# Half of a 31-tap depthwise convolution moved from TensorE to VectorE in a two-layer hybrid block

## The chip, the core and the metric

The kernel runs on one core of a Trainium2 chip. The metric is the time of one execution on the device, in microseconds. A core has five instruction queues that run side by side, each strictly in the order in which its instructions stand: TensorE (PE, matrix products into PSUM; PEld is its weight load), VectorE (DVE), ScalarE (ACT), GpSimd (POOL) and SyncE (SP, which here only issues DMAs). An instruction waits at the head of its queue until what it needs is there, and everything behind it in that queue waits too.

## The reference, cut to what matters

Two layers over 256 tokens of width 1024. Each layer projects the normed input once, runs three branches (differential attention, a convolution branch, a gated delta rule in chunks), gates and adds them, and projects back to the width. The branch that the change touches is

```
u = a * sigmoid(g)                                # a, g: (256, 1024) each, from the input projection
u = causal_depthwise_conv(u, dw_w) + dw_b         # 31 taps, one filter per channel
u = layer_norm(u, ln_w, ln_b)
u = silu(u) * silu(z)
return u @ w_o
```

The convolution of one channel is `out[t] = b + sum over s of w[30-s] * u[t-s]`, for shifts s from 0 to 30. With channels on the 128 partitions and the 256 tokens along the free dimension, a shift is a slice.

## The kernel before, in words

Every projection is a "group" of 512 output columns. A group's weights come as four chunks of 512 KB (`load_chunk`, line 292): one DMA into `w_raw`, then ACT rounds it to `w_hi` (line 303) and DVE forms the remainder `w_lo` (line 304), since a product is made of three passes, hi·hi, hi·lo and lo·hi. Three buffers each of `w_raw`, `w_hi` and `w_lo` rotate. A group has eight k-steps, two per chunk. In `group_a` (channels on the partitions, line 355) a k-step is twelve matmuls of 256 columns, in `group_b` (line 318) six of 512. PSUM accumulators named `acc` rotate through four buffers, two for a group, so that a group can start only when the last but one has been read out.

The order on PE is the order in which the code is written: after each k-step, `pump` (line 270) lets the next due piece of a side stream run (the delta rule's small matmuls, transposes, attention scores). When a piece is due is reckoned by `clk`, a sum of assumed PE times. The other engines' order is made by a scheduler from priorities: `load_chunk` and side streams are raised (`high_priority`), other work stands in program order.

`SEQ` (line 59) lists the groups at the start of a layer: `v` values, `k` delta keys, `c` the convolution's two input groups, `q` and `w` delta queries and values, `d` a convolution group, `x` the start of the delta rule's last stream, `a` attention queries and keys, `z` a gate. The delta rule of one half of the heads (`hs` 0 or 1) has these pieces that appear below: `vp` (three DVE results that PE multiplies with `sel`, lines 667 to 688), the recurrence `dn_z`, `dn_t` (lines 690 to 697), `gf` (line 714), and in `dn_queries` the squares `gx` of the queries, summed by PE against `ones` (line 749), which need both halves of the query group's read-out (`evac_dn`, lines 598 to 608; `big` at line 608 is its end).

The convolution before is done on PE alone. `c_groups(s)` makes `u` for 512 channels in `c_u` and stores it to DRAM (`u_keep`); `conv_load(n)` brings diagonal tap matrices `wd` and four shifted copies `u4` for 256 channels; `conv_group(n)` (line 890) runs 64 small matmuls for each of two blocks of 128 channels into one `acc` tile, and ACT adds the bias on the way to `c_acc` (line 898). There are four such groups in a layer: `d0` and `d1` between the delta groups, `d2` before the last attention groups, and the fourth after the delta rule's output.

Of the kernel before, what the change touches and what calls it, by code (L numbers as in the profile page):

```python
# [10 lines left out]
F32 = mybir.dt.float32  # L11
# [3 lines left out]
AF = mybir.ActivationFunctionType  # L15
ALU = mybir.AluOpType
# [3 lines left out]
P = 128  # L20
T = 256
D = 1024
KT = D // P
GW = 512
DEPTH = 2
# [30 lines left out]
FINE = False  # L56
AHEAD = 600
W_AHEAD = 340
SEQ = "v0 k0 t0 v1 k1 c0 q0 w0 d0 x0 q1 w1 d1 x1 a0 c1 z0 z1 d2 a1".split()
TAPQ = 8  # L60


PC_DB, PC_LW, PC_LB, PC_SC, PC_SUB, PC_DNW = 0, 8, 16, 24, 120, 121
PC_N = 122
PR_AL, PR_DT, PR_LAM = 0, 8, 16
PR_N = 272
CO_ID, CO_NW, CO_TRI, CO_BDU, CO_OFF, CO_BD, CO_E16, CO_IF = 0, 128, 144, 272, 400, 528, 536, 552
# [21 lines left out]
def kernel(  # L89
# [13 lines left out]
    nc = tc.nc  # L103
    V, S, G, TE = nc.vector, nc.scalar, nc.gpsimd, nc.tensor
# [41 lines left out]
        return ap.unsqueeze(1).to_broadcast([ap.shape[0], n, ap.shape[1]])  # L146

    x_keep = dram.tile([T, D], F32, name="x_keep")
    u_keep = dram.tile([D, T], F32, name="u_keep")

    def big():
        return act.tile([P, 2, D], F32, name="big", bufs=3)
# [136 lines left out]
            yield 1.9  # L289

    counter = [0]
    def load_chunk(l, g, c):
        with tc.high_priority(offset=AHEAD + 400 if counter[0] == 0 else W_AHEAD):
            raw = wpool.tile([P, KC, GW], F32, name="w_raw", bufs=3)
            with tc.issue_after(x_dma[1].ins) if counter[0] < NCH else ExitStack():
                nc.sync.dma_start(out=raw, in_=wts[l, g, c])
            hi = wpool.tile([P, KC, GW], F32R, name="w_hi")
            lo = wpool.tile([P, KC, GW], F32R, name="w_lo")
            eng = G if POOL[counter[0] % (NG * NCH)] == "1" else V
            cuts = [slice(k, k + 1) for k in range(KC)] if counter[0] == 0 else [slice(0, KC)]  # L300
            counter[0] += 1
            for kk in cuts:
                S.copy(out=hi[:, kk], in_=raw[:, kk])  # L303
                eng.tensor_sub(out=lo[:, kk], in0=raw[:, kk], in1=hi[:, kk].bitcast(F32))  # L304
        return hi, lo
# [12 lines left out]
    def group_b(l, key, xs, evac, need=()):  # L318
        parts = load_group(l, ORDER.index(key))
        ps = [acc_tile() for _ in range(2)]  # L320
        for k in range(KT):
            for s in need:
                if k == 4 * s[0]:
                    finish(s[1])
            for t in range(2):
                step_b(xs, parts[k // KC], ps, k, t)
            if k == KT - 1:
                evac(ps)
            pump()

    def group_out(l, xs, evacs, need, split):
        parts = {}
# [22 lines left out]
    def group_a(l, key, xs, evac, need=()):  # L355
        xh, xl = xs
        parts = load_group(l, ORDER.index(key))
        ps = [acc_tile().rearrange("p (f t) -> p f t", f=2) for _ in range(2)]
        for c, (hi, lo) in enumerate(parts):
            for kk in range(KC):  # L360
                k = c * KC + kk
                for s in need:
                    if k == 4 * s[0]:
                        finish(s[1])
                for f in range(4):
                    o = ps[f // 2][:, f % 2, :]
                    fs = slice(f * P, (f + 1) * P)
                    last = k == KT - 1 and f % 2 == 1
                    mm(0.108, out=o, lhsT=hi[:, kk, fs], rhs=xh[:, k, :],
                       start=(k == 0 and f % 2 == 0), stop=False)  # L370
                    mm(0.108, out=o, lhsT=hi[:, kk, fs], rhs=xl[:, k, :],
                       start=False, stop=False)
                    mm(0.108, out=o, lhsT=lo[:, kk, fs], rhs=xh[:, k, :],
                       start=False, stop=last)
                    if FINE and f == 1:
                        pump()
                if k == KT - 1:
                    evac(ps)
                pump()

    def transpose4(src, tile_):
        tp = h4(tile_)
# [58 lines left out]
    for l in range(DEPTH):  # L441
# [10 lines left out]

        wbs = lay.tile([P, KT, 32], F32R, name="wbs")
        scw = pc[:, PC_SC:PC_SC + 96]
        ln2 = lay.tile([P, 16], F32, name="ln2")
        ln4 = lay.tile([P, 16], F32, name="ln4")
        nwc = lay.tile([P, 2], F32, name="nwc")
# [15 lines left out]
        def params():  # L473
            V.tensor_scalar(out=scw, in0=scw, scalar1=0.5, scalar2=None, op0=ALU.mult)
            S.copy(out=wbs[:, :, 0:16], in_=wb)
            V.tensor_sub(out=wbs[:, :, 16:32], in0=wb, in1=wbs[:, :, 0:16].bitcast(F32))
            if l == 0:
                masks()
            V.tensor_scalar(out=ln2, in0=pc[:, PC_LW:PC_LW + 16], scalar1=0.5, scalar2=None, op0=ALU.mult)
            V.tensor_scalar(out=ln4, in0=pc[:, PC_LW:PC_LW + 16], scalar1=0.25, scalar2=None, op0=ALU.mult)  # L480
            V.tensor_scalar(out=nwc[:, 0:1], in0=pc[:, PC_SUB:PC_SUB + 1], scalar1=1.0 - lambda_init,
                            scalar2=0.5, op0=ALU.mult, op1=ALU.mult)
            V.tensor_scalar(out=nwc[:, 1:2], in0=pc[:, PC_DNW:PC_DNW + 1], scalar1=0.5, scalar2=None,
                            op0=ALU.mult)
            lamp = sm.tile([P, 2, 64], F32, name="dn_t1", bufs=1)
            lamv = lamr.rearrange("p (a b d) -> p a b d", a=2, b=2)
            V.tensor_tensor(out=lamp, in0=lamv[:, :, 0, :], in1=lamv[:, :, 1, :], op=ALU.mult)
            lams = sm.tile([P, 2], F32, name="lams", bufs=1)
            V.tensor_reduce(out=lams, in_=lamp, axis=AX.X, op=ALU.add)
            lame = sm.tile([P, 2], F32, name="lame", bufs=1)  # L490
            S.activation(out=lame, in_=lams, func=AF.Exp)
            V.tensor_sub(out=nlam, in0=lame[:, 1:2], in1=lame[:, 0:1])
            V.tensor_scalar(out=nlam, in0=nlam, scalar1=-lambda_init, scalar2=None, op0=ALU.add)
# [359 lines left out]
        us = []  # L853

        def c_groups(s):
            tgs = []

            def evac_g(ps):
                for f in range(2):
                    tg = wc()  # L860
                    V.tensor_tensor(out=tg, in0=ps[f], in1=bc_mid(rnb, 2), op=ALU.mult)
                    S.activation(out=tg, in_=tg, func=AF.Tanh, scale=0.5)
                    V.scalar_tensor_tensor(out=tg, in0=tg, scalar=1.0, in1=bc_mid(rnb, 2),
                                           op0=ALU.add, op1=ALU.mult)
                    tgs.append(tg)

            def evac_u(ps):
                u = wk.tile([P, 4, T], F32, name="c_u", bufs=2)
                for f in range(2):
                    ins = V.tensor_tensor(out=u[:, 2 * f:2 * f + 2, :], in0=tgs[f], in1=ps[f],  # L870
                                          op=ALU.mult)
                us.append(u)
                return ins

            group_a(l, ("in", CG + s * GW), H, evac_g)
            group_a(l, ("in", CA + s * GW), H, evac_u)
            nc.sync.dma_start(out=u_keep[s * GW:(s + 1) * GW].rearrange("(a p) t -> p a t", p=P), in_=us[s])
            conv_load(2 * s)

        ac = act.tile([P, 8, T], F32, name="c_acc")  # L880

        def conv_load(n):
            with tc.high_priority(offset=W_AHEAD):
                nc.sync.dma_start(out=wd.rearrange("p f q j c -> p (f q j c)"), in_=cwd[l, n])
                for i in range(4):
                    nc.sync.dma_start(
                        out=u4[32 * i:32 * i + 32, :, i:T],
                        in_=u_keep[n * 2 * P:(n + 1) * 2 * P, 0:T - i].rearrange("(g c) t -> c g t", c=32))

        def conv_group(n):  # L890
            ps = acc_tile().rearrange("p (f t) -> p f t", f=2)
            for f in range(2):
                ct = 2 * n + f
                for q in range(TAPQ):
                    for j in range(4):
                        mm((T - 4 * q) / 2400.0, out=ps[32 * j:32 * j + 32, f, 4 * q:T], lhsT=wd[:, f, q, j, :],
                           rhs=u4[:, 4 * f + j, 0:T - 4 * q], start=(q == 0), stop=(q == TAPQ - 1))
                S.activation(out=ac[:, ct, :], in_=ps[:, f, :], func=AF.Identity, scale=0.5,  # L898
                             bias=pc[:, PC_DB + ct:PC_DB + ct + 1])
                pump()  # L900
            if n in (0, 2):
                conv_load(n + 1)

        def q_group(hs):
            group_a(l, ("in", DQ + hs * GW), H, evac_dn(hs, 1, sts[hs]["kq"][:, :, 1, :]))
# [247 lines left out]
        yc = []  # L1153

        def ln_stream():
            yield 18.6
            pmu = side_tile()
            rsum = gx().rearrange("p (a b) d -> p a (b d)", a=2)
# [184 lines left out]
```

## Time and profile before

| | us |
|---|---|
| median of 3 runs (lowest to highest) | 1106.14 (1105.72 to 1110.63) |
| the profiled execution, its own time | 1110.02 |
| its span | 1108.2 |
| PE busy in the span | 1061.9 |
| DVE busy | 805.4 |
| ACT busy | 550.3 |

The span is the stretch from the first to the last recorded instruction; the 1.8 us beside it lie around it. A row of a timeline gives start, length, engine, line, operation, output and inputs, shapes and count, and in brackets how long the engine had been idle before it and what ended the wait. A row with a count covers several instructions that follow each other closely; its length is from the first start to the last end.

### The profile page before, as it was taken

How to read it: one execution, taken by the hardware profiler on the slowest of the kernel's cores; microseconds unless marked ns; L12 is line 12 of the kernel's file. 1: busy time of each engine (PE TensorE's matmuls, PEld its weight loads, DVE VectorE, ACT ScalarE, POOL GpSimd, SP SyncE). 2: the span in 40 equal slices, each digit the busy share in tenths (PEclk: the TensorE clock that was granted, in tenths of full speed). 3: DMA queues.
4: the chain of work that ended last, by engine and by line, in shares of the span. 5: the costliest groups of instructions: out<-in, count | busy, mean ns of one | idle time of the engine just before them, and what ended most of it. 6: DMA issues, size and time to landing. Idle time of an engine off the chain costs nothing.

```text
span 1108.2 us, 18945 instructions
## 1 busy us (share of the span) xinstructions
PE 1061.9 (96%) x7396; PEld 920.1 (83%) x7396; DVE 805.4 (73%) x1610; ACT 550.3 (50%) x995; POOL 108.0 (10%) x74
## 2 busy tenths in 40 slices
PE   5998899999999999999999989999999999999996
PEld 4998898899687778897889988988987877889785
DVE  4889977586767656687677988767766775757965
ACT  4754544343656544545466534443346564544643
POOL 1022000010010001102102110002000200011130
PEclk9999999999999999998999989999999999999998
DMA  6534653346365555654664454533555543655452
GB/s 211 189 135 134 187 168 125 111 134 171 100 205 172 172 175 185 190 174 155 187 217 152 135 171 136 158 127 98 173 151 155 182 174 119 193 184 189 154 171 96
DMA packets 58266, 177.66 MB, mean 160 GB/s; under 512 B 6592, under 2 KB 17600, under 8 KB 57152
## 3 DMA queue, kind: packets, MB, share of 16 engines
q1 hardware_dynamic: 54592, 171.94, 49.3%
q10 hardware_dynamic: 3584, 4.51, 1.2%
q8 instruction: 58, 0.95, 0.4%
q14 instruction: 32, 0.26, 0.1%
HBM read 172.23 MB, written 4.19 MB: 159 GB/s over the span
## 4 chain that ended last, share of the span: by engine, by line
PE 78%; DVE 14%; ACT 2%; issue 2%; POOL 1%; DMA 1%; ACTq 0%; DVEq 0%
PE acc L249 64%; PE sg L249 9%; DVE w_lo L304 4%; PE sg L253 2%; PE sa L249 2%; DVE wc L604 2%; PE sa L253 1%; ACT w_hi L303 1%; DVE dn_t L695 1%; POOL gf L645 1%; DVE c_acc L1190 1%; DMA cst<-in_consts 1%; DVE dn_z L697 1%; POOL c_acc L1196 0%; DMA pr<-in_prow 0%
## 5 line engine op out<-in xcount | busy, mean ns | idle before, releaser
L304 DVE TENSOR_TENSOR w_lo<-w_raw,w_hi 128x1024 fp32r<-128x1024 f32 (+1 forms) x289 | 361.0, 1250 | 165.9 <-ACT w_hi L303 164.4
L303 ACT CAST w_hi<-w_raw 128x1024 fp32r<-128x1024 f32 (+1 forms) x289 | 302.3, 1047 | 334.6 <-PE acc L249 297.1
L249 PE MATMUL acc<-h_hi,w_hi 128*128 128x256 f32 x768 | 227.9, 297 | 1.8 <-ACT w_hi L303 1.8
L249 PE MATMUL acc<-h_hi,w_lo 128*128 128x256 f32 x768 | 218.9, 285 | 4.5 <-DVE w_lo L304 4.5
L249 PE MATMUL acc<-h_lo,w_hi 128*128 128x256 f32 x768 | 218.1, 284 | 0.0
L249 PE MATMUL acc<-w_hi,h_hi 128*128 128x512 f32 x512 | 209.3, 409 | 2.1 <-ACT w_hi L303 2.1
L249 PE MATMUL acc<-w_lo,h_hi 128*128 128x512 f32 x512 | 200.2, 391 | 2.1 <-DVE w_lo L304 2.1
L249 PE MATMUL acc<-w_hi,h_lo 128*128 128x512 f32 x512 | 200.8, 392 | 0.0
L249 PEld LDWEIGHTS acc<-h_hi,w_lo 128*128 128x128 f32 x768 | 147.9, 193 | 5.7 <-DVE w_lo L304 5.7
L249 PEld LDWEIGHTS acc<-h_hi,w_hi 128*128 128x128 f32 x768 | 148.1, 193 | 2.5 <-ACT w_hi L303 2.0
L249 PEld LDWEIGHTS acc<-h_lo,w_hi 128*128 128x128 f32 x768 | 148.2, 193 | 0.6
L249 PEld LDWEIGHTS acc<-w_hi,h_lo 128*128 128x128 f32 x512 | 96.3, 188 | 21.2
L249 PEld LDWEIGHTS acc<-w_lo,h_hi 128*128 128x128 f32 x512 | 96.8, 189 | 19.3 <-DVE w_lo L304 2.6
L249 PEld LDWEIGHTS acc<-w_hi,h_hi 128*128 128x128 f32 x512 | 96.7, 189 | 19.1 <-ACT w_hi L303 2.5
L249 PE MATMUL acc<-w_hi,y_hi 128*128 128x512 f32 x192 | 78.9, 411 | 1.8 <-ACT wc L1105 1.8
L249 PE MATMUL acc<-w_hi,y_lo 128*128 128x512 f32 x192 | 77.6, 404 | 3.0 <-DVE y_lo L1199 3.0
L249 PE MATMUL acc<-w_lo,y_hi 128*128 128x512 f32 x192 | 76.7, 399 | 0.0
L604 DVE SCALAR_TENSOR_TENSOR wc<-wc,pc 128x255 f32<-128x255 f32 (+1 forms) x144 | 65.9, 498 | 0.0
L249 PE MATMUL acc<-u,wd 128*32 128x256 f32 (+7 forms) x1024 | 55.6, 369 | 0.5 <-ACT c_acc L898 0.5
L1117 POOL TENSOR_TENSOR big<-big,wc 128x512 f32<-128x512 f32 x16 | 28.2, 1786 | 281.8 <-DVE wc L1114 281.8
L929 POOL TENSOR_TENSOR wa<-wa 128x512 f32<-128x512 f32 x16 | 26.3, 1650 | 259.8 <-DVE wa L927 219.1
L249 PEld LDWEIGHTS acc<-u,wd 128*32 128x32 f32 x1024 | 31.6, 110 | 20.3 <-issue 1.8
(297 smaller groups left out, 1438.7 us busy)
## 6 DMA issues: line engine op xcount, KB each, us to landing
w_raw<-in_wts SPq DMA_DIRECT2D x288, 512.0 KB, 3.5
wd<-in_cwd SPq DMA_DIRECT2D x8, 1024.0 KB, 5.5
u_keep<-c_u SPq DMA_DIRECT2D x4, 512.0 KB, 3.1
u<-u_keep SPq DMA_DIRECT2D x8, 256.0 KB, 6.0
u<-u_keep SPq DMA_DIRECT2D x8, 255.0 KB, 6.4
u<-u_keep SPq DMA_DIRECT2D x8, 254.0 KB, 5.9
u<-u_keep SPq DMA_DIRECT2D x8, 253.0 KB, 7.0
big<-in_x SPq DMA_DIRECT2D x4, 256.0 KB, 6.5
```

What stands on the lines that cost most here:

```text
L249: TE.matmul(**kw)
L253: TE.transpose(out=out, in_=in_, identity=ident[0:n, 0:n])
L303: S.copy(out=hi[:, kk], in_=raw[:, kk])
L304: eng.tensor_sub(out=lo[:, kk], in0=raw[:, kk], in1=hi[:, kk].bitcast(F32))
L604: V.scalar_tensor_tensor(out=cv[:, i, s:T], in0=cs[:, i, 0:T - s], scalar=wts_[i][:, 3 - s:4 - s], in1=cv[:, i, s:T], op0=ALU.mult, op1=AL ...
L645: G.tensor_tensor(out=vd, in0=kk, in1=bc_mid(bdu, 4), op=ALU.mult)
L695: V.tensor_tensor(out=t1[:, :, 0:i + 1], in0=z[:, :, 0:i + 1], in1=nrep[:, 0:i + 1, :, i].rearrange("p j c -> p c j"), op=ALU.mult)
L697: V.tensor_reduce(out=z[:, :, i:i + 1], in_=t1[:, :, 0:i + 1], axis=AX.X, op=ALU.add)
L929: G.tensor_tensor(out=ra, in0=ra, in1=rb, op=ALU.add)
L1117: G.tensor_tensor(out=ms, in0=ms, in1=gts[i][t], op=ALU.add)
L1190: V.tensor_scalar(out=pz[:, f, :], in0=pz[:, f, :], scalar1=ln4[:, ct:ct + 1], scalar2=ln4[:, 8 + ct:9 + ct], op0=ALU.mult, op1=ALU.add)
```

## The change

For the first 512 channels of each layer (`c0`) the convolution is now done by DVE, from the `c_u` tile into `c_acc`, with no trip through DRAM: ACT writes the tap without shift and the bias to `c_acc`, then 30 DVE instructions per block of 128 channels multiply a shifted slice of `u` by its tap and add it to `c_acc`, four blocks, 120 instructions a layer. `conv_steps` is a generator; each k-step of the groups that follow calls it once. `d0` and `d1` leave `SEQ`, and with them half of the `wd` matrices and `u4` loads; `d2` and the fourth group stay on PE. The taps join the per-channel table `pc`, which grows from 122 to 246 columns, and are halved once a layer.

```diff
-SEQ = "v0 k0 t0 v1 k1 c0 q0 w0 d0 x0 q1 w1 d1 x1 a0 c1 z0 z1 d2 a1".split()
+SEQ = "v0 k0 t0 v1 k1 c0 q0 w0 x0 q1 w1 x1 a0 c1 z0 z1 d2 a1".split()
...
-PC_N = 122
+PC_N = 122 + 4 * 31
...
             pump()
+            next(steps_[0], None)
...
+            V.tensor_scalar(out=dww, in0=dww, scalar1=0.5, scalar2=None, op0=ALU.mult)
...
             group_a(l, ("in", CA + s * GW), H, evac_u)
-            nc.sync.dma_start(out=u_keep[s * GW:(s + 1) * GW].rearrange("(a p) t -> p a t", p=P), in_=us[s])
-            conv_load(2 * s)
+            if s == 0:
+                steps_[0] = conv_steps()
+                return
+            nc.sync.dma_start(out=u_keep.rearrange("(a p) t -> p a t", p=P), in_=us[s])
+            conv_load(2)
...
+        def conv_steps():
+            for ct in range(4):
+                u = us[0][:, ct, :]
+                w0 = ct * 31
+                S.activation(out=ac[:, ct, :], in_=u, func=AF.Identity, scale=dww[:, w0 + 30:w0 + 31],
+                             bias=pc[:, PC_DB + ct:PC_DB + ct + 1])
+                for sh in range(1, 31):
+                    V.scalar_tensor_tensor(out=ac[:, ct, sh:T], in0=u[:, 0:T - sh],
+                                           scalar=dww[:, w0 + 30 - sh:w0 + 31 - sh],
+                                           in1=ac[:, ct, sh:T], op0=ALU.mult, op1=ALU.add)
+                    yield
...
-            if n in (0, 2):
-                conv_load(n + 1)
+            if n == 2:
+                conv_load(3)
...
         def ln_stream():
+            for _ in steps_[0]:
+                pass
```

Where the steps stand is the scheduler's doing. Three places, all in the first layer (the second has the same); line numbers after the change are some 5 to 22 higher.

DVE, from the end of `c_u` (the convolution's input) over two weight remainders `w_lo`, before: `sse` to `ngam` and `vp` belong to the delta keys of `hs` 1.

```order
L870 TENSOR_TENSOR c_u<-wc,acc 128x512
L656 TENSOR_REDUCE sse<-dn_t_1260 128x8
L304 TENSOR_TENSOR w_lo<-w_raw,w_hi 128x1024
L657 TENSOR_SCALAR sse<-sse 128x8
L659 RECIPROCAL gam<-sse 128x8
...
L665 TENSOR_TENSOR dn_vc<-dn_vc,cst 128x128
L218 SCALAR_TENSOR_TENSOR rs_tk<-rs_tk,sse 128x8
L304 TENSOR_TENSOR w_lo<-w_raw,w_hi 128x1024
L670 CAST vp_1274<-dn_vc 128x128
```

The same place now:

```order
L875 TENSOR_TENSOR c_u<-wc,acc 128x512
L661 TENSOR_REDUCE sse<-dn_t_1261 128x8
L305 TENSOR_TENSOR w_lo<-w_raw,w_hi 128x1024
L897 SCALAR_TENSOR_TENSOR c_acc<-c_u,pc,c_acc 128x255 x2
L897 SCALAR_TENSOR_TENSOR c_acc<-c_u,pc,c_acc 128x254 x2
...
L897 SCALAR_TENSOR_TENSOR c_acc<-c_u,pc,c_acc 128x226 x2
L897 SCALAR_TENSOR_TENSOR c_acc<-c_u,pc,c_acc 128x255
L662 TENSOR_SCALAR sse<-sse 128x8
L305 TENSOR_TENSOR w_lo<-w_raw,w_hi 128x1024
```

All steps of the first two blocks, 60, and the first of the third stand in one piece between two weight remainders, ahead of the delta keys' chain; the third block's others follow between the rows of that chain (10 of them before the last `vp`).

DVE, at the read-out of the delta queries `q0` (`wc<-acc,rnb`, one instruction per accumulator tile), before:

```order
L304 TENSOR_TENSOR w_lo<-w_raw,w_hi 128x1024
L714 TENSOR_TENSOR gf<-sg,ngam 128x512
L598 TENSOR_TENSOR wc<-acc,rnb 128x512 x2
L604 SCALAR_TENSOR_TENSOR wc<-wc,pc 128x255 x2
L695 TENSOR_TENSOR dn_t_1766<-dn_z,o_d 128x8x5
```

The same read-out now, from the first tile to `big`:

```order
L897 SCALAR_TENSOR_TENSOR c_acc<-c_u,pc,c_acc 128x255
L603 TENSOR_TENSOR wc<-acc,rnb 128x512
L700 TENSOR_TENSOR dn_t_1794<-dn_z,o_d 128x8x9
...
L702 TENSOR_REDUCE dn_z<-dn_t_1815 128x8
L603 TENSOR_TENSOR wc<-acc,rnb 128x512
L613 SCALAR_TENSOR_TENSOR big<-wc 128x512
...
L603 TENSOR_TENSOR wc<-acc,rnb 128x512
L613 SCALAR_TENSOR_TENSOR big<-wc 128x512
```

The two tiles of `q0` were read out one after the other; now the second comes after the whole recurrence `dn_z` and three weight remainders. From the first weight remainder of the place above to the second `big`, 99 convolution steps and 8 weight remainders stand on DVE.

PE, at the former `d0`, before (`acc<-h_hi` and the like are k-steps, `sg<-cst` a transpose of the delta keys):

```order
L253 MATMUL sg<-cst,t_1256 128x128 x4
L249 MATMUL acc<-u_80,wd 32x256 x4
...
L249 MATMUL acc<-u_80,wd 32x228 x4
L249 MATMUL sg<-ones,gx 128x1 x8
L249 MATMUL acc<-u_80,wd 32x256 x4
```

The same place now:

```order
L253 MATMUL sg<-cst,t_1257 128x128 x4
L249 MATMUL acc<-h_hi,w_hi 128x256
...
L249 MATMUL acc<-h_hi,w_lo 128x256
L249 MATMUL sg<-ones,gx 128x1 x8
L249 MATMUL acc<-h_hi,w_hi 128x256
```

The two halves of `d0` are gone, and one k-step of the next group, `q1`, now stands ahead of the sums of `gx`.

## Rows read from the trace of the kernel before

**Rows 1.** Page, part 1: busy us, share of span, instructions.

```profile
PE 1061.9 (96%) x7396; PEld 920.1 (83%) x7396; DVE 805.4 (73%) x1610; ACT 550.3 (50%) x995; POOL 108.0 (10%) x74
```

**Rows 2.** Busy us of each engine in a stretch, then PE clock, DMA share.

```profile
100.00:120.00 20.00, 16.47 (x145) 15.58 (x144) 19.15 (x53) 5.61 (x8) 4.83 (x4) 1.00 0.72 202
640.00:660.00 20.00, 16.54 (x117) 15.61 (x116) 17.00 (x47) 4.77 (x5) 4.83 (x4) 0.83 0.76 213
```

**Rows 3.** Timeline of PE, 105 to 118 us: start, length, what, idle before.

```profile
106.07 0.39 PE L249 MATMUL acc<-h_hi,w_lo 128*128 128x256 f32 x1 [1.12 <-DVE w_lo L304]
...
112.61 0.23 PE L249 MATMUL sg<-vp,sel 128*128 128x128 bf16 x1 [1.59 <-DVE vp L670]
113.19 1.04 PE L249 MATMUL sg<-vp,sel 128*128 128x128 bf16 x11 [0.35 <-DVE vp L672]
```

**Rows 4.** Groups by line: count, busy us, mean ns, idle before.

```profile
L604 DVE SCALAR_TENSOR_TENSOR wc<-wc,pc 128x255 f32<-128x255 f32 (+1 forms) x144 | 65.9, 498 | 0.0
L249 PE MATMUL acc<-u,wd 128*32 128x256 f32 (+7 forms) x1024 | 55.6, 369 | 0.5 <-ACT c_acc L898 0.5
...
L1068 DVE SCALAR_TENSOR_TENSOR o_d<-o_d,rs_yo,wa 128x128 f32<-128x128 f32 x32 | 8.7, 347 | 0.0
...
L898 ACT ACTIVATE c_acc<-acc,pc 128x256 f32<-128x256 f32 x16 | 7.6, 472 | 21.1 <-PE acc L249 20.7
...
L474 DVE TENSOR_SCALAR pc<-pc 128x96 f32<-128x96 f32 x2 | 0.4, 200 | 0.0
```

**Rows 5.** Timeline of PE, 130 to 150 us: `d0` and the sums.

```profile
136.63 3.47 PE L249 MATMUL acc<-u,wd 128*32 128x256 f32 x64
140.03 1.95 PE L249 MATMUL sg<-ones,gx 128*128 128x1 f32 x16
141.91 3.47 PE L249 MATMUL acc<-u,wd 128*32 128x256 f32 x64
```

**Rows 6.** Timeline of DVE, 108 to 147 us: ends of the stretch, every wait.

```profile
109.43 0.16 DVE L657 TENSOR_SCALAR sse<-sse 128x8 f32<-128x8 f32 x1
...
116.72 1.23 DVE L304 TENSOR_TENSOR w_lo<-w_raw,w_hi 128x1024 fp32r<-128x1024 f32 x1 [0.51 <-ACT w_hi L303]
...
126.99 0.69 DVE L608 SCALAR_TENSOR_TENSOR big<-wc 128x512 f32<-128x512 f32 x1 [0.76 <-ACT wc L607]
127.93 1.23 DVE L304 TENSOR_TENSOR w_lo<-w_raw,w_hi 128x1024 fp32r<-128x1024 f32 x1 [0.24 <-ACT w_hi L303]
...
134.07 1.23 DVE L304 TENSOR_TENSOR w_lo<-w_raw,w_hi 128x1024 fp32r<-128x1024 f32 x1 [0.52 <-ACT w_hi L303]
...
140.42 1.66 DVE L604 SCALAR_TENSOR_TENSOR wc<-wc,pc 128x254 f32<-128x254 f32 x2
```

**Rows 7.** Timeline of DVE, 162 to 168 us: four taps in a row.

```profile
163.65 1.66 DVE L604 SCALAR_TENSOR_TENSOR wc<-wc,pc 128x255 f32<-128x255 f32 x4
```

**Rows 8.** Line 604 alone: ns shortest/median/longest, first and last start.

```profile
L604 DVE SCALAR_TENSOR_TENSOR wc<-wc,pc x144: 471/478/1277, 46.7 to 728.3; 128x255 f32<-128x255 f32 x48, 128x254 f32<-128x254 f32 x48, 128x253 f32<-128x253 f32 x48
```

**Rows 9.** Timeline of DVE, 638 to 655 us (second layer).

```profile
648.33 0.16 DVE L657 TENSOR_SCALAR sse<-sse 128x8 f32<-128x8 f32 x1
```

**Rows 10.** Timeline of PE, 676 to 690 us (second layer).

```profile
682.98 1.95 PE L249 MATMUL sg<-ones,gx 128*128 128x1 f32 x16
```

**Rows 11.** Busy us by stretch, then PE clock (second layer).

```profile
648.00:652.00 4.00, 1.83 (x12) 1.37 (x12) 3.96 (x21) 1.05 (x1) 0.00 (x0) 0.91 0.82 260
652.00:656.00 4.00, 3.84 (x23) 3.67 (x23) 2.96 (x13) 0.59 (x1) 0.00 (x0) 0.50 1.04 232
656.00:660.00 4.00, 4.00 (x28) 4.00 (x28) 2.14 (x3) 1.04 (x1) 0.00 (x0) 0.74 1.10 308
660.00:668.00 8.00, 8.00 (x78) 7.91 (x78) 7.59 (x23) 4.82 (x10) 0.00 (x0) 1.00 0.16 62
```

**Rows 12.** Timeline of ACT, 96 to 150 us.

```profile
119.18 0.91 ACT L601 ACTIVATE wc<-wc,pc 128x256 f32<-128x256 f32 x2 [2.49 <-DVE wc L598]
...
124.57 0.63 ACT L742 ACTIVATE gx<-big 128x512 f32<-128x512 f32 x1 [0.57 <-DVE big L608]
```

**Rows 13.** Chain of waits, 100 to 200 us: one k-step.

```profile
150.67 1.43 PE acc L249 x12
```

More of the change, by code (lines that the diff above doesn't have):

```diff
@@ L58 @@
 W_AHEAD = 340
-SEQ = "v0 k0 t0 v1 k1 c0 q0 w0 d0 x0 q1 w1 d1 x1 a0 c1 z0 z1 d2 a1".split()
+SEQ = "v0 k0 t0 v1 k1 c0 q0 w0 x0 q1 w1 x1 a0 c1 z0 z1 d2 a1".split()
 TAPQ = 8
-PC_DB, PC_LW, PC_LB, PC_SC, PC_SUB, PC_DNW = 0, 8, 16, 24, 120, 121
-PC_N = 122
+PC_DB, PC_LW, PC_LB, PC_SC, PC_SUB, PC_DNW, PC_DW = 0, 8, 16, 24, 120, 121, 122
+PC_N = 122 + 4 * 31
 PR_AL, PR_DT, PR_LAM = 0, 8, 16
@@ L148 @@
     x_keep = dram.tile([T, D], F32, name="x_keep")
-    u_keep = dram.tile([D, T], F32, name="u_keep")
+    u_keep = dram.tile([GW, T], F32, name="u_keep")
     def big():
@@ L291 @@
     counter = [0]
+    steps_ = [iter(())]
     def load_chunk(l, g, c):
@@ L379, in group_a @@
                 pump()
+                next(steps_[0], None)
     def transpose4(src, tile_):
@@ L454 @@
         scw = pc[:, PC_SC:PC_SC + 96]
+        dww = pc[:, PC_DW:PC_DW + 124]
         ln2 = lay.tile([P, 16], F32, name="ln2")
@@ L876, in c_groups @@
             group_a(l, ("in", CA + s * GW), H, evac_u)
-            nc.sync.dma_start(out=u_keep[s * GW:(s + 1) * GW].rearrange("(a p) t -> p a t", p=P), in_=us[s])
-            conv_load(2 * s)
-        ac = act.tile([P, 8, T], F32, name="c_acc")
+            if s == 0:
[3 more added lines that the diff above has]
+            conv_load(2)
+        ac = act.tile([P, 8, T], F32, name="c_acc")
+        def conv_steps():
[9 more added lines that the diff above has]
+                    yield
         def conv_load(n):
             with tc.high_priority(offset=W_AHEAD):
-                nc.sync.dma_start(out=wd.rearrange("p f q j c -> p (f q j c)"), in_=cwd[l, n])
+                nc.sync.dma_start(out=wd.rearrange("p f q j c -> p (f q j c)"), in_=cwd[l, n - 2])
                 for i in range(4):
@@ L887, in conv_load @@
                         out=u4[32 * i:32 * i + 32, :, i:T],
-                        in_=u_keep[n * 2 * P:(n + 1) * 2 * P, 0:T - i].rearrange("(g c) t -> c g t", c=32))
+                        in_=u_keep[(n - 2) * 2 * P:(n - 1) * 2 * P, 0:T - i].rearrange("(g c) t -> c g t", c=32))
         def conv_group(n):
@@ L1313 @@
          chan(a["conv_ln_b"], 8), chan(a["dn_conv_w"], 24),
-         chan(a["attn_subln_w"], 1), chan(a["dn_norm_w"], 1)], axis=2)
+         chan(a["attn_subln_w"], 1), chan(a["dn_norm_w"], 1),
+         chan(a["conv_dw_w"][:, :, :GW], 4)], axis=2)
     taps = np.zeros((DEPTH, 4 * TAPQ, D), np.float32)
     taps[:, :31] = a["conv_dw_w"][:, ::-1]
-    taps = taps.reshape(DEPTH, TAPQ, 4, 4, 2, 4, 32)
-    cwd = np.zeros((DEPTH, 4, 4, 32, 2, TAPQ, 4, 32), np.float32)
+    taps = taps[:, :, GW:].reshape(DEPTH, TAPQ, 4, 2, 2, 4, 32)
+    cwd = np.zeros((DEPTH, 2, 4, 32, 2, TAPQ, 4, 32), np.float32)
     for c in range(32):
         cwd[:, :, :, c, :, :, :, c] = taps[..., c].transpose(0, 3, 2, 4, 1, 5)
-    cwd = cwd.reshape(DEPTH, 4, P, 2 * TAPQ * 4 * 32)
+    cwd = cwd.reshape(DEPTH, 2, P, 2 * TAPQ * 4 * 32)
     prow = np.concatenate(
```

## The prediction

> **What bounds the kernel now.** I read the busy times first [rows 1]: PE is busy for 96% of the span, DVE for 73%. Over the whole, work taken from PE counts in full and DVE has 300 us to spare. Then the stretches: where the new steps would fall, the averages don't hold. From 100 to 120 us DVE is busy for 19.15 of 20 us and PE for 16.47; the second layer has the same place at 640 to 660 [rows 2]. Third, PE's timeline there: it waits for the weight remainder w_lo and, at 112.61, for vp, both made by DVE, with no stock in hand [rows 3]. So in these stretches DVE sets the pace, and they begin with the very weight remainder behind which the order now puts 61 convolution steps.
>
> **What a step costs.** The nearest instruction is the short convolution's tap at line 604: same operation, a scalar per partition, both inputs in SBUF, 253 to 255 columns. Four in a row, two alternating chains as in the new order, take 1.66 us and one alone 0.478 (median) [rows 7, 8]: a step every (1.66 - 0.48) / 3 = 0.393 us. The new ones are 255 down to 226 columns long, 240.5 on average; from 128 columns (0.347) to 254 (0.478) a column is worth 1.0 ns [rows 4, 8], so 0.379 us. A layer's 120 take 45.5 us. Bounds: 0.272, what a tap of 128 columns keeps DVE busy (8.7 / 32), and 0.498, the mean length of line 604 with no overlap [rows 4].
>
> On the overlap the Trainium skill says otherwise: "VectorE: DVE Perf Modes", section "The DRAIN you can't avoid", has the next operation start only when the pipe has emptied. By that rule a step would cost its whole length, 0.464, and the forecast below would be 17 us higher (2 x 99 x 0.085). The four in 1.66 us speak against it.
>
> **What PE loses and gains, step by step.** Removed: half of the convolution's matmuls. A block of 64 takes 3.40 us from its start to the next row's [rows 5]; 1024 / 64 = 16 blocks [rows 4], 8 go: 27.2 us.
>
> Added: the wait. I follow DVE from the end of that w_lo (109.43 [rows 6]) to the second `big` of q0's read-out, because PE's sums of gx need it and everything behind them on PE waits in order.
> - 99 convolution steps: 37.5 us.
> - The other instructions of this piece are those that ran from 109.43 to the start of 140.42 before: 31.0 us, less the 2.03 us in which DVE waited (0.51 + 0.76 + 0.24 + 0.52), less two taps that now come later (0.8): 28.2 us [rows 6].
> - ACT between: a wait for tanh as before `big` at 126.99 (0.8), then the square (0.63), behind some 0.4 of the taps' first products [rows 6, 12]: 1.8 us.
>
> So the sums start at 109.4 + 37.5 + 28.2 + 1.8 = 176.9 us, against 140.03 [rows 5]: 36.9 us late. PE can't use this time: it is stopped first at vp (71 steps ahead of it), later at q1's first k-step, whose accumulator is freed only by the late second read-out of q0. From the sums on PE has less to do than before: three blocks of convolution (10.2 us) and one k-step (1.4 us [rows 13]) that ran ahead. Side pieces change places but not in number. Net, before the clock: 25.3 us.
>
> The clock: in the second layer 2 us of idle time are followed by a granted clock of 0.50 and 0.74 over 8 us, then 1.00 [rows 11]: 8 x 0.38 = 3.0 us lost at the lower of the two levels, 1.2 GHz. After the new waits I add the same. First layer +28.3 us. Second layer: the piece starts at 648.33 and the sums stood at 682.98 [rows 9, 10]; 648.3 + 67.5 = 715.8 is 32.8 us late, less 11.6, plus 3.0: +24.2 us. The rest of DVE's steps (21) lie beside PE's next fifteen k-steps (21 us) and side pieces, and just fit.
>
> Priced at nothing: on ACT 8 bias reads of 0.47 go and 8 first taps come [rows 4], and ACT is half idle [rows 1]; halving the taps is 0.2 us of DVE [rows 4], in a part where PE doesn't wait for it, at most 0.5 in all if it does; `pc` doubles in size, at worst a fraction of a microsecond ahead of the first groups; of SP's queue only issues go, none is put ahead of a weight load, and since DVE and not a transfer ends the waits of [rows 3], fewer transfers give nothing, at most the waits for w_hi (0.51 + 0.24 + 0.52 in [rows 6]).
>
> **Sum.** 28.3 + 24.2 = 52.5 us. The profiled execution took 1110.0 (span 1108.2 and 1.8 around it), which makes 1162.5; it was 3.9 us above the median of the runs, and the changed kernel will be timed as a median, so 1106.1 + 52.5 = 1159 us.
>
> **Rivals.**
> - *The steps are hidden, and PE is the bound.* For it: DVE's 300 idle us, and one step to a k-step, 0.38 beside 1.43 us, would fit in most of the layer. Then only the 27.2 us count: 1079 us, faster. Against it: the order on DVE, which is fixed, has 61 in a row where [rows 3] show PE without stock. It needs a step of little weight: the delay is 198 steps (two layers) less 22.4 us, so it turns to a gain below 0.113 us a step, and no row of this kind is under 0.272.
> - *Only the block of 61 counts.* PE waits for vp, 71 x 0.379 = 26.9 us, and what DVE still has behind it hides under PE's own work. Then a layer costs 26.9 less 13.6, plus the clock in the first: 16.3 + 13.3 = 30, 1136 us. For it: my later waits are reckoned on a DVE without any other gap. Against: eight weight remainders lie in that chain, and between vp and the sums PE has only 12 k-steps (17 us) and a few small pieces of its own.
> - *The clock stays low.* If waits keep returning up to the end of w1, the 32 us of PE's work from the sums on run at half the rate, up to 29 us a layer more: 1217 us. Against: full clock 8 us after the wait [rows 11]. The Trainium skill, "TensorE: Matmul & The Clock Gate", "Part 1: The HAM clock gate", states that an idle engine is throttled and steady work releases it; the trace agrees (0.50, 0.74, 1.00).
>
> **How the numbers follow.** My forecast 0.84, hidden 0.04, only the block 0.08, low clock 0.04. The forecast's own range: with the step at 0.272 it is 21 us lower, at 0.498 it is 24 us higher: 1138 to 1183. The second rival takes the low end to 1132; the others are left out. A measurement tells apart about 0.5%, 5.5 us. Faster 0.04, within it 0.01 (a few values between the rivals), slower 0.95.
>
> **What would show it.** In the profile after: a row of some 60 steps on DVE lasting about 23 us from 109 us on and again near 680; behind it on PE one wait of 25 us or more for vp, then one for an accumulator and one for gx; mean step 0.38 us apart; total PE busy about 27 us less, idle about 80 more. Right in sum and wrong in cause, if the waits on PE came from ACT or from DMA. Wrong, if weight remainders run between the 60, or if PE has no wait over 5 us there.

## The result

| | median, us | ratio to before (95% interval) |
|---|---|---|
| before (4 runs beside it) | 1108.39 | |
| changed | 1146.11 (1145.96 to 1146.71) | 1.0336 [1.0317, 1.0356] |

The change makes the kernel 37.7 us slower. The forecast was 1159 us, 52.5 us slower: the direction and the place were right, the loss was put about 15 us too high.

The profiled execution took 1145.96 us, its span is 1144.2. Page, part 1 of the kernel after, with the columns of [rows 1]:

```profile
PE 1036.1 (91%) x6884; PEld 909.5 (79%) x6884; DVE 886.8 (78%) x1852; ACT 551.3 (48%) x995; POOL 105.1 (9%) x74
```

PE is busy for 25.8 us less and idle for 108.1 us instead of 46.3, 61.8 more where about 80 had been expected. The stretches of 20 us that answer to [rows 2] (length, then busy time of PE, PEld, DVE, ACT and POOL, then PE clock, DMA share, GB/s):

```profile
100.00:120.00 20.00, 9.99 (x80) 9.39 (x78) 19.86 (x44) 5.51 (x8) 4.82 (x4) 0.83 0.25 79
120.00:140.00 20.00, 0.58 (x3) 0.26 (x4) 20.00 (x61) 0.00 (x0) 0.00 (x0) 0.50 0.10 27
160.00:180.00 20.00, 10.98 (x62) 10.40 (x61) 18.35 (x47) 5.68 (x11) 2.51 (x2) 0.69 0.22 67
180.00:200.00 20.00, 20.00 (x167) 20.00 (x167) 19.93 (x44) 9.79 (x15) 0.00 (x0) 0.97 0.32 107
680.00:700.00 20.00, 2.73 (x17) 2.41 (x18) 20.00 (x61) 0.59 (x1) 0.00 (x0) 0.50 0.10 27
```

From 120 to 140 us PE does almost nothing and DVE is never idle; the second layer repeats it. The timeline of DVE says with what (answers to [rows 6]: start, length, what):

```profile
108.65 1.28 DVE L305 TENSOR_TENSOR w_lo<-w_raw,w_hi 128x1024 fp32r<-128x1024 f32 x1
109.85 23.27 DVE L897 SCALAR_TENSOR_TENSOR c_acc<-c_u,pc,c_acc 128x255 f32<-128x255 f32 x61
133.03 0.17 DVE L662 TENSOR_SCALAR sse<-sse 128x8 f32<-128x8 f32 x1
133.11 1.22 DVE L305 TENSOR_TENSOR w_lo<-w_raw,w_hi 128x1024 fp32r<-128x1024 f32 x1
```

61 steps stand in one piece, 23.27 / 61 = 0.381 us from start to start, and behind them the row that came at 109.43 before ([rows 6]) comes at 133.03. What PE waited for in the whole span (total, times, longest), the rows that are new or larger:

```profile
PE sg L249 <- DVE vp L675: 53.7, 2, 26.8
PE acc L249 <- DVE wc L603: 10.9, 2, 5.5
...
PE sg L249 <- ACT gx L747: 7.5, 3, 3.5
```

And where, on the timeline of PE (in brackets the idle time before and what ended it; answers to [rows 3, 5]):

```profile
138.28 0.29 PE L249 MATMUL sg<-vp,sel 128*128 128x128 bf16 x1 [26.84 <-DVE vp L675]
...
168.92 0.58 PE L249 MATMUL acc<-h_hi,w_hi 128*128 128x256 f32 x1 [5.45 <-DVE wc L603]
...
170.66 1.87 PE L249 MATMUL sg<-ones,gx 128*128 128x1 f32 x8
...
176.00 1.87 PE L249 MATMUL sg<-ones,gx 128*128 128x1 f32 x8 [3.47 <-ACT gx L747]
```

The three waits stand in the order of the forecast: vp, an accumulator, gx. The sums now come in two halves, with a piece of a k-step between them.

### The profile page after: what moved, and what is told of

Read it like the earlier page. It is cut to its first block, busy times and chain, and to the rows that moved or that the text cites. A ratio compares the mean times of both kernels' runs of the same rounds, so it can differ in the third digit from the quotient of the medians.

```text
span 1144.2 us, 18135 instructions
## 1 busy us (share of the span) xinstructions
PE 1036.1 (91%) x6884; PEld 909.5 (79%) x6884; DVE 886.8 (78%) x1852; ACT 551.3 (48%) x995; POOL 105.1 (9%) x74
## 4 chain that ended last, share of the span: by engine, by line
PE 76%; DVE 18%; issue 2%; ACT 2%; DMA 1%; POOL 1%; ACTq 0%; DVEq 0%
PE acc L249 61%; PE sg L249 10%; DVE c_acc L897 6%; DVE w_lo L305 4%; PE sa L249 2%; PE sg L253 2%; DVE wc L609 2%; PE sa L253 2%; DVE dn_t L700 1%; DVE c_acc L1212 1%; DMA cst<-in_consts 1%; ACT w_hi L304 1%; DVE big L613 1%; DVE dn_z L702 1%; DVE wc L603 0%
## 5 line engine op out<-in xcount | busy, mean ns | idle before, releaser
L249 PE MATMUL acc<-h_hi,w_hi 128*128 128x256 f32 x768 | 230.7, 300 | 10.9 <-DVE wc L603 10.9
L897 DVE SCALAR_TENSOR_TENSOR c_acc<-c_u,pc,c_acc 128x255 f32<-128x255 f32 (+14 forms) x240 | 103.0, 469 | 0.1
L249 PE MATMUL acc<-w_hi,y_lo 128*128 128x512 f32 x192 | 75.2, 392 | 3.0 <-DVE y_lo L1221 3.0
L609 DVE SCALAR_TENSOR_TENSOR wc<-wc,pc 128x255 f32<-128x255 f32 (+2 forms) x144 | 64.0, 477 | 0.0
L249 PE MATMUL sg<-vp,sel 128*128 128x128 bf16 (+3 forms) x192 | 11.9, 210 | 56.0 <-DVE vp L675 53.7
L249 PEld LDWEIGHTS <-sel 128*128 128x128 bf16 x192 | 9.0, 102 | 57.6 <-DVE vp L675 54.1
```

What stands on the lines that cost most here:

```text
L249: TE.matmul(**kw)
L609: V.scalar_tensor_tensor(out=cv[:, i, s:T], in0=cs[:, i, 0:T - s], scalar=wts_[i][:, 3 - s:4 - s], in1=cv[:, i, s:T], op0=ALU.mult, op1=AL ...
L897: V.scalar_tensor_tensor(out=ac[:, ct, sh:T], in0=u[:, 0:T - sh], scalar=dww[:, w0 + 30 - sh:w0 + 31 - sh], in1=ac[:, ct, sh:T], op0=ALU.m ...
```

## The experiments

Two landmarks serve all runs: the first read-out of `c_u` (start of the trouble) and the first read-out of a0, `wa<-acc,cosr`. In the kernel before and in the run without steps, the parts of the span outside this stretch differ by less than 2 us each, so the stretch holds the difference.

**Without the steps.**

```diff
-                for sh in range(1, 31):
+                for sh in range(1, 1):
...
-                    yield
+                yield
```

> The 240 steps on VectorE are left out (of half the channels only the first tap is computed); everything else is as in the changed kernel. Theory (the steps delay the work behind them on DVE): the two waits for vp of 26.8 us are gone, the sums of gx stand near 140 us again, and PE has 11.6 us less to do behind them in each layer: 1108.4 - 23.2 = 1085 us. If all of PE's removed 27.2 us count: 1081. Rival (PE lost the two convolution blocks that it had as filling in a stretch in which DVE sets the pace, and the steps only take idle time): most of the loss stays, 1125 us or more.

Measured: 1070.42 us, 0.9656 [0.9624, 0.9689] of before. The steps are the loss; no part of it comes from the missing filling. The gain of TensorE's lighter load, 36.6 us, was larger than either number expected. The stretch between the landmarks, one row a layer, first in the kernel before, then without steps:

```profile
106.10:203.10 97.00, 92.94 (x905) 83.61 (x906) 76.07 (x169) 42.23 (x67) 4.54 (x4) 1.00 0.53 159
645.00:746.00 101.00, 97.05 (x904) 87.69 (x905) 76.26 (x169) 42.19 (x67) 4.46 (x4) 0.95 0.50 153
```

```profile
107.50:186.40 78.90, 75.61 (x612) 72.55 (x613) 73.17 (x166) 41.36 (x64) 4.77 (x4) 0.98 0.43 134
628.20:706.50 78.30, 75.86 (x612) 72.84 (x613) 72.45 (x166) 41.47 (x64) 4.82 (x4) 0.98 0.44 136
```

Before, PE fills the stretch (93 of 97 us) and DVE has 21 us to spare. Without the convolution blocks PE and DVE are both near its length: there is no room left on either. Of the 40.8 us by which the two stretches are shorter, 8 blocks of 3.47 us are 27.8; the rest (less waiting, a clock of 0.98 instead of 0.95 in the second, 36 small matmuls a layer that now stand behind the stretch, 208 on `sg` in it in place of 244) was not divided further here.

**Steps late and spread.** `conv_steps` starts with a0, and each step is queued on DVE behind the weight remainder of its own chunk (`w_done` lists the instructions that make the remainders):

```diff
+    def conv_step(k):
+        with tc.issue_after(w_done[k // KC - NCH]):
+            next(steps_[0], None)
...
-                steps_[0] = conv_steps()
...
             if hs == 0:
                 finish(s_k[0])
+                steps_[0] = conv_steps()
```

> All 240 steps are computed, but a layer's 120 begin with the attention groups (a0), one for each k-step, and each is queued on DVE behind the weight remainder of its own chunk. Theory (the place in DVE's order is what costs): no step stands ahead of vp or of the sums of gx, DVE has 72 us of idle time between 180 and 400 us, so the time is that of the run without steps and a few us: 1085 to 1092. Rival (DVE lacks the room: 45.5 us a layer cost what they cost wherever they stand): slower than the kernel before, 1115 us or more.

Measured: 1079.14 us, 0.9746 [0.9709, 0.9784]: faster than both kernels, with all the steps computed. DVE is busy for 890.8 us, as much as in the changed kernel, so it isn't the amount of work over the whole span that costs.

**Spread from q0 on.** The same spreading, but the steps start where the change starts them.

> The steps begin where they began in the changed kernel (with q0), one for each k-step, but each is queued behind the weight remainder of its chunk: 5 steps stand ahead of the last vp and 15 ahead of the second read-out of q0, in place of 71 and 99. Theory (each step ahead of the sums delays them by its 0.38 us): 15 x 0.38 = 5.7 us a layer over the run without steps, 1085 + 11 = 1096 us. Rival 1 (only steps ahead of vp count): 5 x 0.38 = 1.9 a layer, 1089 us. Rival 2 (DVE's room): 1115 us or more, since DVE is at 18 to 19 of 20 us here.

Measured: 1101.92 us, 0.9944 [0.9925, 0.9963]. This is none of the three numbers; it is 31.5 us above the run without steps, where the 15 steps ahead of the sums explain 11.

```profile
107.10:196.00 88.90, 78.05 (x614) 74.56 (x615) 86.72 (x207) 41.29 (x63) 4.63 (x4) 0.92 0.39 119
```

This is the first layer's stretch. It holds some 41 more DVE instructions than without steps (207 against 166), and DVE is busy for all but 2.2 us of it. So a step costs here even when it stands behind vp and behind the sums. That gave the theory that the next runs test: in this stretch DVE itself is the bound.

**All 120 in one piece.** Written down with a0, but not held back:

```diff
-                steps_[0] = conv_steps()
...
             if hs == 0:
                 finish(s_k[0])
+                steps_[0] = conv_steps()
```

> The steps are written down with the attention groups, but nothing holds them back on DVE: the scheduler puts all 120 of a layer in one piece behind the same weight remainder, ahead of vp, and none later. Theory: one wait of PE for vp of 120 x 0.38 = 45.6 us a layer, and no late read-out; sums of gx 8.0 us later than in the changed kernel (120 steps ahead of them in place of 99): 1146 + 16 = 1162 us. Rival (the block alone decides, the steps behind it were hidden): 61 + 10 steps ahead of vp become 120, 18.6 us more a layer, 1146 + 37 = 1183 us. Rival (DVE's room, not the order): 1146 us, the same as the changed kernel.

Measured: 1163.03 us, 1.0494 [1.0460, 1.0529]: the theory's 1162. DVE's timeline has

```profile
108.97 45.66 DVE L896 SCALAR_TENSOR_TENSOR c_acc<-c_u,pc,c_acc 128x255 f32<-128x255 f32 x120
```

and PE waits 48.1 us for vp in each layer. The place within the stretch does count, but it is worth 17 us between this order and the changed kernel's, of some 76 that the steps cost there.

**Dense: 120 in the stretch, but 8 ahead of vp.** The edit is shown against the run of steps spread from q0 on.

```diff
         with tc.issue_after(w_done[k // KC - NCH]):
-            next(steps_[0], None)
+            for _ in range(4):
+                next(steps_[0], None)
```

> As the run of spread steps, but four steps for each k-step, so that all 120 of a layer again stand before the first read-out of a0's groups; ahead of the last vp stand 8, ahead of q0's second read-out 33 (71 and 99 in the changed kernel), behind it 51 in one piece. Theory now (from c_u to the first read-out of a0, DVE itself is the bound: that stretch lasts as long as DVE is busy in it and 2 to 7 us, with or without steps, so every step in it costs its 0.38 us wherever it stands): 1146 us, as the changed kernel, within 6. Rival 1 (only steps ahead of the sums of gx count): 1070 + 2 x 33 x 0.38 = 1095 us. Rival 2 (only steps ahead of vp count): 1070 + 2 x 8 x 0.38 = 1076 us.

Measured: 1145.97 us, 1.0331 [1.0301, 1.0361]: the changed kernel's time, with almost nothing ahead of vp. Both rivals fall. The stretch of the first layer, and two of PE's waits in the whole span:

```profile
107.60:224.20 116.60, 82.30 (x616) 78.13 (x617) 113.86 (x279) 41.61 (x63) 6.36 (x4) 0.84 0.30 92
```

```profile
PE acc L249 <- DVE wc L611: 42.7, 4, 20.7
...
PE sg L249 <- DVE vp L683: 7.1, 2, 3.5
```

The 26.8 us for vp became 20.7 us for an accumulator that DVE reads out. Removing the wait for vp moved it; DVE's sum in the stretch stayed.

**Half of the steps.**

```diff
+                n = 31 if ct < 2 else 1
...
-                for sh in range(1, 31):
+                for sh in range(1, n):
```

> Of the four channel tiles two are left out (only their first tap is computed): 60 steps a layer in place of 120, all before the first read-out of a0; ahead of the last vp now stand 11, ahead of q0's second read-out 38. Theory (DVE's sum in the stretch decides): DVE is busy for 73 + 22.8 = 95.8 us in it, the stretch lasts 98 to 101 us against 78.6 without steps: 1070 + 2 x 21 = 1112 us (1108 to 1116). Rival 1 (sums of gx): 1070 + 2 x 38 x 0.38 = 1099 us. Rival 2 (vp alone): 1078 us.

Measured: 1104.73 us, 0.9964 [0.9941, 0.9988]: between the theory's 1112 and the first rival's 1099, and below the theory's range of 1108 to 1116.

```profile
107.60:204.30 96.70, 81.02 (x612) 76.97 (x613) 93.29 (x225) 40.87 (x63) 4.54 (x4) 0.89 0.36 110
```

DVE's busy time came as expected less 2.5 us (93.3 against 95.8), and the stretch is 3.4 us longer than that: DVE is nearly full again. The expected price was too high since the run without steps had 5.7 us of DVE's idle time in the stretch, which the first steps use up. By itself this run doesn't tell the two apart.

All stretches side by side (steps ahead of the last vp and in the stretch by DVE's order; us of layer 1 / layer 2):

| run | ahead of vp | in it | length | PE busy | DVE busy |
|---|---|---|---|---|---|
| before | 0 | 0 | 97.0 / 101.0 | 92.9 / 97.1 | 76.1 / 76.3 |
| no steps | 0 | 0 | 78.9 / 78.3 | 75.6 / 75.9 | 73.2 / 72.5 |
| late, spread | 0 | 12 | 78.3 / 78.2 | 75.0 / 74.9 | 75.4 / 75.3 |
| spread from q0 | 5 | 44 | 88.9 / 90.0 | 78.1 / 79.1 | 86.7 / 87.0 |
| half | 11 | 60 | 96.7 / 95.8 | 81.0 / 81.7 | 93.3 / 92.8 |
| dense | 8 | 120 | 116.6 / 118.3 | 82.3 / 83.9 | 113.9 / 114.1 |
| changed | 71 | 120 | 117.9 / 119.4 | 80.6 / 81.7 | 115.4 / 116.0 |
| in one piece | 120 | 120 | 125.6 / 125.8 | 75.8 / 76.9 | 118.7 / 117.9 |

From 44 steps on the length follows DVE's busy time, 2 to 4 us above it; only where all 120 stand ahead of vp is it 7 to 8, probably since PE then still has work of its own when DVE has done.

**The steps added and nothing removed.** What was TensorE's lighter load worth in the changed kernel? From the kernel before: steps in, `d0` and `d1` kept, their results thrown away.

```diff
...
-                S.activation(out=ac[:, ct, :], in_=ps[:, f, :], func=AF.Identity, scale=0.5,
+                S.activation(out=ac[:, ct, :] if n > 1 else wc()[:, 0, :], in_=ps[:, f, :],
+                             func=AF.Identity, scale=0.5,
...
```

> The kernel before with the 240 steps added and nothing removed: TensorE computes all eight convolution groups, but the results of d0 and d1 are thrown away and those of the steps used. DVE's order is that of the changed kernel (61 in a piece, 71 ahead of vp, 99 ahead of the second read-out). It measures what PE's lighter load gave in the changed kernel. As forecast (11.6 us a layer): 1146 + 23 = 1169 us. If the removal is worth there what it is worth without steps (36.6 us): 1183 us. If DVE is the bound up to the first read-out of a0, PE's blocks lie in its waits: 1146 to 1152 us.

Measured: 1195.69 us, 1.0791 [1.0770, 1.0813], above all three. The edit had brought a wait of its own: for a free `wc` buffer ACT had to wait for DVE's late read-outs, and PE for ACT:

```profile
PE acc L249 <- ACT wc L918: 16.1, 4, 6.3
```

So it was run again with another place for the thrown-away results:

```diff
-                S.activation(out=ac[:, ct, :] if n > 1 else wc()[:, 0, :], in_=ps[:, f, :],
+                S.activation(out=ac[:, ct if n > 1 else ct + 4, :], in_=ps[:, f, :],
```

> As the run with the steps added and nothing removed, but the thrown-away results of d0 and d1 go to rows of c_acc that ACT itself overwrites later, no longer to a wc buffer, for which ACT had to wait (PE stood 16.1 us behind it there). If that wait explains what was above the changed kernel beyond the blocks: 1195.7 - 16.1 = 1180 us, so TensorE's lighter load was worth some 34 us in the changed kernel, about what it was worth without steps (36.6). By the forecast's own term (11.6 us a layer): 1169 us. If DVE is the bound up to the first read-out of a0 and PE's blocks lie in its waits: 1146 to 1152 us.

Measured: 1179.23 us, 1.0651 [1.0635, 1.0667], where 1180 was expected. The steps alone cost 72 us; taking four blocks a layer from PE gave 1179.2 - 1146.1 = 33.1 us back, not the 23.2 of the forecast. It also speaks against a pure DVE bound, under which it would be 1146 to 1152: here the stretches last 133.7 and 135.6 us with DVE busy for 119.6 and 119.9, so that behind the sums PE's order sets the end.

**Starting later.** Steps from c1 on, spread as before.

```diff
+            if s == 1:
+                steps_[0] = conv_steps()
...
-                steps_[0] = conv_steps()
```

> As the run of late steps, but a layer's steps begin 16 k-steps later, with the second convolution gate (c1): none stands before the read-outs of a0. If the 2.7 us a layer for which PE waited for the rotated queries came from steps beside the read-outs of a0: 1074 us. If steps cost something anywhere DVE runs beside PE: 1079 us, the same.

Measured: 1078.69 us, 0.9745 [0.9710, 0.9781]: the same as from a0 on (the four runs lie between 1076.9 and 1084.8). My suspicion was wrong: the 2.8 us wait is still there, at 323 us in this run, and belongs to the read-outs of a1, between which steps still stand. The run without steps and the changed kernel, in which no step stands there, don't have it.

**Six of eight blocks of channels late.** The edit is shown against the run from c1 on; `d2` also leaves `SEQ`.

```diff
-            for ct in range(4):
-                u = us[0][:, ct, :]
+            for ct in range(6):
+                u = us[ct // 4][:, ct % 4, :]
...
-            next(steps_[0], None)
+            for _ in range(2):
+                next(steps_[0], None)
...
```

> Late steps taken further: six of the eight channel tiles on VectorE (180 steps a layer, two for each k-step from c1 on), one convolution group left on TensorE. If DVE has room behind the read-outs of a0: two more groups of 3.47 us per 64 matmuls leave PE, 4 x 3.47 = 13.9 us less than the run that begins with c1: 1065 us. If DVE's room ends there (45.5 + 22.8 us of steps beside some 70 us of idle time up to the layer norm's place): 1079 to 1095 us.

Measured: 1071.76 us, 0.9685 [0.9662, 0.9708]: 7 us faster than from c1 with four, half of the 13.9. It is the fastest full version here.

```profile
PE 1017.7 (95%) x6628; PEld 891.3 (83%) x6628; DVE 918.6 (86%) x1972; ACT 551.4 (52%) x995; POOL 105.6 (10%) x74
```

## Why the prediction was right in sign and 15 us too high

**Price of a step: right.** 0.379 us was forecast; the pieces give 23.27 / 61 = 0.381 and 45.66 / 120 = 0.381. Its length is another thing:

```profile
L897 DVE SCALAR_TENSOR_TENSOR c_acc<-c_u,pc,c_acc x240: 445/462/1265, 109.9 to 762.9; 128x255 f32<-128x255 f32 x6, 128x253 f32<-128x253 f32 x6, 128x251 f32<-128x251 f32 x6, 128x249 f32<-128x249 f32 x6
```

A step lasts 0.462 us (median, the middle of the three) and the next starts 0.381 after it. This holds for the order of these pieces, in which the steps of two blocks alternate (255, 255, 254, 254 columns and so on), so that none reads what the one right before it wrote. Where steps of one block follow each other, as in the run from c1 on, each reads the accumulator that the one before wrote:

```profile
309.02 1.46 DVE L905 SCALAR_TENSOR_TENSOR c_acc<-c_u,pc,c_acc 128x239 f32<-128x239 f32 x3
```

These three start 0.50 us apart, (1.46 - 0.46) / 2, each only after the one before has ended; the median of 82 such pairs in that run is 0.498. The Trainium skill, "VectorE: DVE Perf Modes", section "The DRAIN you can't avoid", has the next instruction start only once the pipe is empty, and adds that one that is not held starts earlier. The trace has both: 0.498 us in one chain, 0.381 in two that alternate. The prediction quoted the first half alone; it took the right price because it took it from alternating taps.

**Late sums: right within 1 to 2 us.** They were forecast at 176.9 in the first layer; the second half started at 176.00. The end of the sums moved from 141.98 ([rows 5]) to 177.87, 35.9 us (forecast 36.9); in the second layer from 684.93 ([rows 10]) to 736.95, less the 21.4 of the first layer: 30.6 (forecast 32.8). Inside the second layer the delay is 32.6: its first read-out of `c_u` is only 19.4 us later (645.03 before, 664.42 after), so 2.0 us came back between the two stretches.

**The clock: about two thirds.** From the end of the sums to the first read-out of a0 PE is busy without a gap in all three kernels that matter. Busy PE, its clock and DMA (the first layer): before, the run with nothing removed, and the changed kernel:

```profile
141.98:203.10 61.12, 61.12 (x583) 1.00 0.46 140
```

```profile
177.22:239.90 62.68, 62.68 (x582) 0.97 0.46 137
```

```profile
177.87:224.50 46.63, 46.63 (x343) 0.96 0.36 114
```

The first two do the same work, so the low clock behind the waits costs 62.68 - 61.12 = 1.6 us (2.3 in the second layer), not 3.0. The longer waits end before the sums, so that part of the slow time probably fell on work that would have waited for gx anyway.

**The step that failed** is "From the sums on PE has less to do than before: three blocks of convolution (10.2 us) and one k-step", with "Side pieces change places but not in number" priced at nothing. The relief is 62.68 - 46.63 = 16.1 us in the first layer and 63.33 - 46.85 = 16.5 in the second, not 11.6. The blocks themselves were priced right: before, they keep PE busy for 10.35 us of the stretch. In the run with nothing removed, the first row behind the sums is

```profile
177.15 5.03 PE L249 MATMUL acc<-u,wd 128*32 128x256 f32 x64
```

That is 5.03 us in place of 3.47 ([rows 5]), at the low clock. But this slow time does not go with the block: in the changed kernel a k-step stands there and takes 2.56 us, from 177.87 to 180.43, in place of 1.43 ([rows 13]). With the k-step's 1.4, 4.3 us of the 16.1 remain for the other matmuls that are gone from the stretch. Of the 583 - 343 = 240, 192 are the blocks', 12 the k-step's and 36 small ones of side streams, on `sg`. What PE does on `sg` in the stretch, before and then after:

```profile
141.98:203.10 61.12, 20.76 (x152) 1.00 0.46 140
```

```profile
177.87:224.50 46.63, 16.27 (x116) 0.96 0.36 114
```

The 36 that are missing now stand behind the first read-out of a0 (at 203.06 before, 224.46 after). One of the pieces, before and after:

```profile
196.27 1.05 PE L249 MATMUL sg<-gx,t 128*128 128x128 f32 x8
```

```profile
224.96 1.05 PE L249 MATMUL sg<-gx,t 128*128 128x128 f32 x8
```

From `c_u` to the end of the sums PE did 92 on `sg` in both kernels, so "PE can't use this time" was right. Behind the read-out the pieces cost nothing: the parts of the span outside the two stretches add up to 906.9 us in the changed kernel and to 907.9 in the run with nothing removed, and PE is idle there for 33.0 us in place of 38.0. Their number stayed, as forecast; that their place could be worth 4 us a layer was left out. Why they come later was not tested; `pump` reckons when a piece is due by assumed PE times, and the removed blocks no longer add to these.

With the measured terms, layer 1 is 35.9 - 16.1 + 1.6 = 21.4 and layer 2 is 30.6 - 16.5 + 2.3 = 16.4: 37.8 us, against 37.7 measured. The profiled executions differ by 36.0 us in span, since behind the second stretch the changed kernel is 1.8 us shorter; that the terms meet the medians to 0.1 us is chance. Of the 14.7 us too many, 9.3 are the relief, 3.2 the delay of the sums (2.0 of it between the stretches), 2.2 the clock. The range of 1138 to 1183 us was made from the price of a step alone, which was right; the terms that were off had no range of their own, so it is partly luck that 1146 lies inside.

**The reason: half right.** That 99 steps ahead of the sums delay them is what the traces show for this order. But the dense run costs the same with 33 ahead of them. The better reason is wider: from `c_u` to the read-outs of a0 DVE has less than 6 us to spare once PE is lighter, and a step costs there wherever it stands. *Hidden* (1079 us) fell for this order, yet its number came out for the late one (1079.1), by another sum: 1070.4 without steps and 8.7 for the steps. *Only the block counts* (1136 us) fell: the waits of 5.5 and 3.5 us behind vp are real, and without the block (dense) the time is the same. *The clock stays low* fell: 0.97 from 180 to 200 us.

Open: why six blocks gave only half of their 13.9 us. PE's waits for the attention weights (`a_pe`) are 5.4 us there, against 2.3 in the run with four from c1 on, but nothing was tried on them.

## What to carry to other kernels

Find the stretch into which a scheduler will pull ready work, and add up there what the receiving engine does: idle time elsewhere (300 us here) can't be used by work that is ready early, unless something in the code holds it back. When one engine's busy time fills a stretch, reordering within it mostly turns one wait into another (26.8 us for vp into 20.7 for an accumulator); moving the work out of it is what helped, 1146 to 1079 us. Test what work that is taken away is worth by putting it back: here it was 33 us where the forecast said 23, mostly because small work of other streams moved too, to a place where it cost nothing.

## What the runs showed of the hardware that was not expected

- Steps on DVE that alternate between two accumulators start 0.381 us apart although each lasts 0.462, 120 times in a row. Steps that each read the accumulator that the one right before wrote start 0.498 us apart (median of 82 pairs in the run from c1 on), 0.035 after the end of the one before.
- The same 64 matmuls of a convolution block took 3.47 us before and 5.03 us right behind a wait of 3.5 us and the sums, in the run with nothing removed; the granted clock from 160 to 180 us there was 0.75.
